# A hybrid decoder step on one core: another order of work in the first stage

## The chip, the core and the metric

The kernel runs on one core of a Trainium2 chip. The core has a tensor engine (PE, with its weight loads shown apart as PEld), a vector engine (DVE), a scalar engine (ACT, also called ScalarE), GpSimd (POOL) and a queue engine (SP), and 16 DMA engines that all queues share. Each engine works through its own list of instructions in order and waits at semaphores for the others. The metric is the device time of one execution in microseconds: 1053.73 us, the median of three runs (1053.68 to 1057.52).

## What is computed

One layer of a decoder, for 512 prompt tokens and 8 x 4 sample tokens; 544 columns in all, and 1024 features.

```python
def trunk_layer(x, c, mixer, lp):
    ada = jnp.einsum('bd,dn->bn', jax.nn.silu(c), lp['w_ada']) + lp['b_ada']
    sh_m, sc_m, gt_m, sh_f, sc_f, gt_f = [a[:, None, :] for a in jnp.split(ada, 6, axis=-1)]
    h = rms_norm(x, g[0]) * (1.0 + sc_m) + sh_m
    y, st = mixer(h)                      # one input projection, then two mixers
    x = x + gt_m * rms_norm(y, g[1])
    h = rms_norm(x, g[2]) * (1.0 + sc_f) + sh_f
    a, b = jnp.split(jnp.einsum('btd,df->btf', h, lp['w_ffn_in']), 2, axis=-1)
    x = x + gt_f * rms_norm(jnp.einsum('btf,fd->btd', jax.nn.silu(a) * b, lp['w_ffn_out']), g[3])
```

The mixer projects h to queries, six kinds of keys and values, gates, the two halves of a gated linear unit (glu) and merge gates. One branch is attention over compressed blocks, selected blocks and a window; for the samples the cached pages come from a pool through a page table. The other is a 31-tap convolution over the glu's output. Compressing means a small network over 32 consecutive key or value rows.

## The kernel before

Data lie transposed: features on the 128 partitions, tokens along the columns, so x is eight blocks of 128 x 544. The columns are two halves of 272 (HT); the last 32 are the samples. Products are made in split form: a value is rounded to a high part (ACT: hi, L168), the rest is the low part (DVE: lo, L171), and high x high, high x low and low x high are summed in PSUM. A weight tile of eight 128 x 128 blocks so takes 24 products per half.

Weights come over SP's queue in the order of one table (RING, made by _plan): 8 conditioning tiles (ada), 3 glu tiles, 8 more ada tiles, and then all others. The first 19 use three buffers wraw and five buffers araw. A load is issued as soon as its buffer is free, strictly in the table's order; after the 19 the two tables w1t of the compressing network follow (load_w1, L440).

The order of instructions has two sources. Later stages are events with due times in microseconds of a plan (ev, spawn, L120 to L143), run in the order of these times. Within that, the building layer places instructions on each engine by its own priorities, and an instruction may be pinned behind another on its engine (tc.issue_after).

The first stage (L470 to L576) goes like this. x is loaded, ACT squares it, DVE sums the squares (acc), PE sums over partitions, and rs, the reciprocal root, is made for all columns (rstd_from, L374). Meanwhile ada tiles arrive. conditioning(h), L511, makes half h of shift and scale, for row blocks 4h to 4h+3: eight tiles of four products with silu(c) into one PSUM tile (ada_product), copied by ACT (adaz, L319), turned by PE (L325), bias added by DVE (adaT, L335), and A0 = (1 + scale) x gain (L527). Dummy products (warm, L491), whose results nothing reads, keep PE busy in the waits. rows(k), L555, makes row block k for each half of the columns: DVE xn = x * A * rs (L405), ACT hh = round(xn + shift) (L407), DVE hl = xn + shift - hh (L408). norm_samples (L410) does the samples of four blocks at once. opened(k), L559, makes the 18 products of block k for the first three glu tiles, whose split weights are w0h and w0l, in six PSUM banks held open over all eight blocks. The loop at L567 runs conditioning(1) between the products of blocks 3 and 4.

Gathers run on POOL: load_pages(bq), L446, issues eight indirect DMAs for page group bq, into the tile X. Group 0 stands behind a tiny copy (pace, L550) that reads ada tile 14, so its gathers wait for that tile; group 1 is called at L575 with no such pin. compress_pages (L454) later multiplies the pages of a group with w1t, 16 products for keys and 16 for values.

After the first stage come the other glu tiles (ztile), key and value tiles (kv_tile), the convolution on DVE (conv, L638), and the samples' queries (q_sample, L840: PE, an ACT copy qz, PE again). compress_prompt, L760, copies the prompt's keys and values with 16 ACT instructions into Xc (L773), ordered so that each of 16 positions l is a contiguous block of 64 columns (four heads x 16 blocks), and multiplies them with w1t, Xc being the operand that PE loads (L778).

## Time and profile before

| | |
|---|---|
| median of three runs | 1053.73 us |
| profiled execution | 1054.71 us, span 1052.9 us |
| PE busy | 1015.9 us (96%) |
| DVE, ACT, POOL busy | 726.8, 529.5, 169.3 us |
| first 50 us: PE, DVE, ACT busy | 44.3, 18.1, 15.9 us |
| first 50 us: DMA share, rate | 0.97, 363 GB/s |
| 50 to 240 us: PE, DVE, ACT busy | 175.9, 138.4, 66.1 us |
| fourth glu tile's first product | 69.35 us |

The profile names an instruction by its line, engine and operation and by its tiles, out<-in. An fp32 product shows as two records. A bracket at the end of a row is the idle time of the engine ahead of the instruction, and what ended it. PE's busy time counts pipelined products and dummies alike, so it doesn't tell how far PE got; the start times of certain products do.

### The profile page before, as it was taken

Reading aid. Unit: us, or ns where it says so; the run is one execution under the profiler, and the core shown is the slowest. Engines: PE = TensorE matmul, PEld = TensorE weight load, DVE = VectorE, ACT = ScalarE, POOL = GpSimd, SP = SyncE. Lnnn points to the kernel's source line nnn. Section 1 sums busy time; section 2 is a strip of 40 time slices with the busy share of each in tenths; the row PEclk is TensorE's granted clock in tenths of the full one; section 3 lists DMA queues with packets and bytes.
Section 4 is the critical chain, followed back from the end, with each engine's and each line's share of the span. In section 5 each row is a group of like instructions: output and inputs, shape, how many; then the busy total and the mean of one; then the engine's idle time right before and its main releaser. Section 6 shows DMA issues by size and latency. Waiting matters only on the chain.

```text
span 1052.9 us, 21049 instructions
## 1 busy us (share of the span) xinstructions
PE 1015.9 (96%) x8454; PEld 918.6 (87%) x8454; DVE 726.8 (69%) x1351; ACT 529.5 (50%) x1169; POOL 169.3 (16%) x175
## 2 busy tenths in 40 slices
PE   8889899899999999999999899999999999999996
PEld 7789788799986787777787499999999999999996
DVE  2469989334386677676765767899888888544644
ACT  3242112646555455654643556765666666544442
POOL 4331530000225243353431000000000000000000
PEclk9999999999999999999999999999999999999998
DMA  9943685433624524424334555655233333555652
GB/s 341 376 151 100 216 263 180 149 115 84 210 62 145 176 99 151 152 99 165 123 120 152 187 184 183 195 190 168 93 101 101 101 101 101 212 181 169 205 178 87
DMA packets 50001, 167.55 MB, mean 159 GB/s; under 512 B 6208, under 2 KB 8400, under 8 KB 49520
## 3 DMA queue, kind: packets, MB, share of 16 engines
q1 hardware_dynamic: 36432, 122.57, 34.8%
q0 software_dynamic: 6272, 22.42, 6.5%
q10 hardware_dynamic: 7200, 21.22, 5.6%
q8 instruction: 66, 1.08, 0.4%
q14 instruction: 31, 0.25, 0.1%
HBM read 149.38 MB, written 16.81 MB: 158 GB/s over the span
## 4 chain that ended last, share of the span: by engine, by line
PE 78%; DVE 10%; DMA 6%; ACT 3%; issue 2%; POOL 1%; SPq 0%; ACTq 0%; DVEq 0%
PE mm L165 48%; PE big L165 10%; PE pv L165 9%; DVE cy L658 6%; PE pt L165 5%; PE big L1083 4%; DMA wraw<-in_wall_dram 3%; DMA araw<-in_wall_dram 1%; DVE wl L171 1%; ACT Xc L773 1%; DMA X<-in_rows_dram,idx 1%; DMA x<-in_xT_dram 1%; ACT PB L1055 1%; POOL X L431 1%; DMA vw<-in_vwin_dram 1%
## 5 line engine op out<-in xcount | busy, mean ns | idle before, releaser
L168 ACT ACTIVATE wh<-wraw 128x1024 fp32r<-128x1024 f32 (+1 forms) x183 | 166.0, 909 | 181.8 <-PE mm L165 100.8
L171 DVE TENSOR_TENSOR wl<-wraw,wh 128x1024 fp32r<-128x1024 f32 (+1 forms) x135 | 156.2, 1158 | 131.8 <-ACT wh L168 115.4
L165 PE MATMUL mm<-hh,wh 128*128 128x272 f32 (+1 forms) x608 | 172.8, 311 | 4.9 <-ACT zt L740 3.5
L165 PE MATMUL mm<-hl,wh 128*128 128x272 f32 (+1 forms) x608 | 168.3, 304 | 0.0
L165 PEld LDWEIGHTS mm<-hh,wh 128*128 128x128 f32 x608 | 116.7, 192 | 16.5 <-issue 6.4
L165 PEld LDWEIGHTS mm<-hl,wh 128*128 128x128 f32 x608 | 116.2, 191 | 5.6 <-issue 2.6
L165 PE MATMUL mm<-hh,wl 128*128 128x272 f32 (+1 forms) x608 | 100.5, 303 | 0.0
L165 PEld LDWEIGHTS mm<-hh,wl 128*128 128x128 f32 x608 | 85.8, 190 | 5.8 <-issue 2.8
L1055 ACT ACTIVATE PB<-big,mx 128x128 f32<-128x128 f32 (+3 forms) x128 | 66.0, 526 | 48.6 <-DVE mx L1052 42.7
L165 PE MATMUL mm<-uh,wh 128*128 128x272 f32 x352 | 90.2, 288 | 0.0
L165 PE MATMUL mm<-ul,wh 128*128 128x272 f32 x352 | 90.1, 288 | 0.0
L658 DVE SCALAR_TENSOR_TENSOR cy<-hist,vc,cy 128x512 f32<-128x512 f32 x120 | 88.0, 789 | 0.4
L165 PE MATMUL mm<-h2h,wh 128*128 128x272 f32 x328 | 77.4, 288 | 0.0
L1063 POOL TENSOR_SCALAR PB<-PB,mx 128x128 f32<-128x128 f32 (+3 forms) x56 | 59.6, 1078 | 84.8 <-DVE mx L1060 50.8
L165 PE MATMUL mm<-h2l,wh 128*128 128x272 f32 x260 | 66.5, 287 | 0.0
L165 PEld LDWEIGHTS mm<-uh,wh 128*128 128x128 f32 x352 | 66.4, 189 | 0.0
L165 PEld LDWEIGHTS mm<-ul,wh 128*128 128x128 f32 x352 | 66.2, 188 | 0.0
L165 PEld LDWEIGHTS mm<-h2h,wh 128*128 128x128 f32 x328 | 58.5, 188 | 0.0
L165 PE MATMUL mm<-h2h,wl 128*128 128x272 f32 x312 | 53.3, 288 | 0.5 <-ACT pv L1550 0.5
L165 PE MATMUL mm<-uh,wl 128*128 128x272 f32 x352 | 52.2, 288 | 0.0
L1052 DVE TENSOR_REDUCE mx<-big 128x2 f32<-128x256 f32 (+3 forms) x64 | 50.6, 815 | 0.4
L165 PEld LDWEIGHTS mm<-h2l,wh 128*128 128x128 f32 x260 | 48.9, 188 | 0.0
(481 smaller groups left out, 2273.0 us busy)
## 6 DMA issues: line engine op xcount, KB each, us to landing
wraw<-in_wall_dram SPq DMA_DIRECT2D x174, 512.0 KB, 4.2
araw<-in_wall_dram SPq DMA_DIRECT2D x12, 512.0 KB, 10.3
wraw<-in_wall_dram SPq DMA_DIRECT2D x16, 384.0 KB, 3.6
xraw<-in_wall_dram SPq DMA_DIRECT2D x8, 512.0 KB, 6.3
kw<-in_kwin_dram ACTq DMA_DIRECT2D x8, 512.0 KB, 3.6
out_wk_dram<-kw ACTq DMA_DIRECT2D x8, 512.0 KB, 4.6
vw<-in_vwin_dram ACTq DMA_DIRECT2D x8, 512.0 KB, 3.5
out_wv_dram<-vw ACTq DMA_DIRECT2D x8, 512.0 KB, 2.6
```

Source lines behind the costliest of these rows:

```text
L165: pe.matmul(out, lhsT, rhs, start=start, stop=stop, **more)
L168: act.activation(dst, src, AF.Copy, scale=scale)
L171: (eng or dve).tensor_sub(dst, src, h.bitcast(F32))
L431: pool.indirect_dma_start(out=X[:, pg], out_offset=None, in_=rows2, in_offset=bass.IndirectOffsetOnAxis(ap=idx[:, 0, col:col + 1], axis=0))
L658: dve.scalar_tensor_tensor(y, hist[:, ct, k:k + TP], w, y, op0=OP.mult, op1=OP.add)
L773: act.activation(o, src[:, r], AF.Copy)
L1052: dve.tensor_reduce(mx[:, 0, r, 2 * jj:2 * jj + 2], sc[:, :, :w], axis=AX.X, op=OP.max, negate=True)
L1055: act.activation(P[r][:, :, j * 128:j * 128 + 128], sc[:, jp, :w].rearrange("p (k n) -> p k n", n=128), AF.Exp, bias=mx[:, 0, r, j:j + 1], ...
L1063: (dve if r or g == 3 and i > 1 else pool).tensor_scalar(v, v, m[:, j:j + 1], None, op0=OP.mult)
L1083: pe.transpose(p[:, x, j * 128:j * 128 + 128], P[r][:, kt, j * 128:j * 128 + 128], ident)
```

## The change

In the first stage:

- x is multiplied by the root in place, once, before any block of rows (eight DVE products of 544 columns).
- ACT then makes hh straight from x, as round(A * x + shift), and DVE makes the same value unrounded (xt) for the low part. The samples' block drops its product with the root.
- conditioning(h) is cut into cond_tile(h, k) and cond_end(h). The tiles of the second half are called behind the blocks' products: two behind block 0, three behind block 1, two behind block 2, one behind the rows of block 3, whose products are pinned behind the second half's turning on PE (issue_after). Then blocks 4 to 7 follow.
- Dummy products go: nine ahead of the first half, three each behind its tiles 1 to 3, and all ten of the second half.
- load_pages(1) stands behind the last gather of load_pages(0), so also behind the pace copy.

Xc is laid out by head and token, so ACT writes 256 contiguous columns per copy, and PE's operand for position l takes every 16th column. Some due times of the plan move, by up to 6 us of the plan; the convolution's taps are spaced 0.966 instead of 1.196.

```diff
-        def conditioning(h):
-            p = P_pt()
-            for k in range(8):
-                raw, tag = take("ada", 8 * h + k)
-                ada_product(p, k, raw)
-                if h and k == 6:
-                    paced(0, raw[:, 0:1])
-                if h == 0 and 0 < k < 7:
-                    warm(3, raw[:, 0:128])
-                raw_done(tag)
-            z = ada_quarters(p)
-            wb = pw if h == 0 else P_pv()
-            warm(3, raw[:, 0:128], wb[:, 0:128])
-            ada_first(h, z)
-            warm(7, z[:, 0:128], wb[:, 0:128])
+        def cond_tile(h, k):
+            if k == 0:
+                cond[h] = P_pt()
+            raw, tag = take("ada", 8 * h + k)
+            ada_product(cond[h], k, raw)
+            if h == 0 and 3 < k < 7:
+                warm(3, raw[:, 0:128])
+            if h and k == 6:
+                paced(0, raw[:, 0:1])
+            if h == 0 and k == 7:
+                warm(3, raw[:, 0:128])
+            raw_done(tag)
+
+        def cond_end(h):
+            z = ada_quarters(cond[h])
+            turned = ada_first(h, z)
+            if h == 0:
+                warm(7, z[:, 0:128])
...
-        warm(9, wt)
-        conditioning(0)
+        for k in range(8):
+            dve.tensor_mul(x0[:, k], x0[:, k], rs)
+        for k in range(8):
+            cond_tile(0, k)
+        cond_end(0)
...
             with tc.issue_after(pool.tensor_copy(pace[:, bq:bq + 1], seen).ins):
-                load_pages(bq)
+                last = load_pages(bq)
+            with tc.issue_after(last):
+                load_pages(bq + 1)
...
-            for hf in range(2):
-                norm_rows(p0, k, hf, x0[:, k], rs, A0, adaT[:, 0], hh, hl, hS)
+            a, sh = A0[:, k, 0:1], adaT[:, 0, k, 0:1]
+            xt = p0.tile([128, TP], F32, name="xt", tag="xt", bufs=2)
+            dve.tensor_scalar(xt, x0[:, k, 0:TP], a, sh, op0=OP.mult, op1=OP.add)
+            for sl in (slice(0, HT), slice(HT, TP)):
+                act.activation(hh[:, k, sl], x0[:, k, sl], AF.Identity, bias=sh, scale=a)
+                dve.tensor_sub(hl[:, k, sl], xt[:, sl], hh[:, k, sl].bitcast(F32))
...
-        for h in range(2):
-            if h:
-                conditioning(1)
-            for k in range(4 * h, 4 * h + 4):
-                rows(k)
-                if k == 4 * h:
-                    norm_samples(p0, k, x0, rs[:, T - NS:], A0, adaT[:, 0], hh, hl, hS[:, k:k + 4])
+        for k, (a, b) in enumerate(((0, 2), (2, 5), (5, 7), (7, 8))):
+            block(k)
+            if k < 3:
                 opened(k)
-        load_pages(1)
+            for j in range(a, b):
+                cond_tile(1, j)
+        with tc.issue_after(cond_end(1)):
+            opened(3)
+        for k in range(4, 8):
+            block(k)
+            opened(k)
...
-        spawn(t, conv(ct, max(t, 40.379 + 29.131 * ct), 1.196))
+        spawn(t, conv(ct, max(t, 40.379 + 29.131 * ct), 0.966))
...
-        Xc = xp.tile([128, 2, 16, 64], F32, name="Xc", tag="X1")
+        Xc = xp.tile([128, 2, 4, 256], F32, name="Xc", tag="X1")
...
-                    src = zts[kd, pr][64 * h2:64 * h2 + 64, 0:TP].rearrange("p (b l r) -> p r b l", b=16, r=2)
+                    src = zts[kd, pr][64 * h2:64 * h2 + 64, 0:TP].rearrange("p (t r) -> p r t", r=2)
                     for r in range(2):
-                        o = Xc[64 * r:64 * r + 64, kd, :, g * 16:g * 16 + 16].rearrange("p l b -> p b l")
+                        o = Xc[64 * r:64 * r + 64, kd, g]
                         act.activation(o, src[:, r], AF.Copy)
         yield t + 26.409
         p = P_pt()
+        Xl = Xc.rearrange("p k g (b l) -> p k l (g b)", l=16)
         for l in range(16):
             for kd in range(2):
-                mm(p[64 * kd:64 * kd + 64, 0:128], Xc[:, kd, l], w1t[kd][:, l], l == 0, False)
+                mm(p[64 * kd:64 * kd + 64, 0:128], Xl[:, kd, l], w1t[kd][:, l], l == 0, False)
```

What this does to the engines' lists shows at three places. The first is POOL at the gathers (X) of the first stage; before:

```order
L484 MEMSET h1v 128x1024
L580 MEMSET QB 128x512
L431 DMA X<-in_rows_dram,idx 128x512 x8
L550 COPY pace<-araw 128x1
L431 DMA X<-in_rows_dram,idx 128x512 x8
```

With the change, at the same place of POOL's list:

```order
L484 MEMSET h1v 128x1024
L612 MEMSET QB 128x512
L559 COPY pace<-araw 128x1
L430 DMA X<-in_rows_dram,idx 128x512 x16
L622 MEMSET Vn 128x512
```

The eight gathers that stood ahead of the pace copy now stand behind the eight others.

The second place is PE at the second half's conditioning. There pt<-araw,cs and pt<-wraw,cs are ada products, mm and big the open glu banks, pt<-c,adaz is the turning, and pv<-wraw,hl and pv<-adaz,hl are dummies. Before, from the end of block 3 to the first products of block 4:

```order
L165 MATMUL big<-hl,w0h 128x272 x4
L165 MATMUL pt<-wraw,cs 32x256 x3
L165 MATMUL pt<-araw,cs 32x256 x8
L165 MATMUL pt<-wraw,cs 32x256 x4
L165 MATMUL pt<-araw,cs 32x256 x8
L165 MATMUL pt<-wraw,cs 32x256 x4
L165 MATMUL pv<-wraw,hl 128x128 x3
L325 MATMUL pt<-c,adaz 128x128 x2
L165 MATMUL pv<-adaz,hl 128x128 x7
L165 MATMUL mm<-hh,w0h 128x272
L165 MATMUL big<-hh,w0h 128x272 x2
```

With the change, from within block 2 to the first products of block 3:

```order
L165 MATMUL mm<-hh,w0l 128x272
L165 MATMUL pt<-wraw,cs 32x256 x4
L165 MATMUL mm<-hh,w0l 128x272
L165 MATMUL big<-hh,w0l 128x272 x4
L165 MATMUL mm<-hl,w0h 128x272 x2
L165 MATMUL big<-hl,w0h 128x272 x4
L165 MATMUL pt<-araw,cs 32x256 x8
L165 MATMUL pt<-wraw,cs 32x256 x4
L325 MATMUL pt<-c,adaz 128x128 x2
L165 MATMUL mm<-hh,w0h 128x272 x2
L165 MATMUL big<-hh,w0h 128x272 x4
```

The ada products of the second half stand between the blocks, the dummies are gone, and a whole block of products follows the turning.

The third place is PE where the first page products (pv<-X,w1t) stand. Before, that was within block 4:

```order
L165 MATMUL mm<-hh,w0h 128x272
L165 MATMUL mm<-hh,w0l 128x272
L165 MATMUL pv<-X,w1t 128x128
L165 MATMUL mm<-hh,w0h 128x272
L165 MATMUL big<-hh,w0h 128x272 x2
```

With the change it is behind block 7, ahead of the fourth glu tile (mm<-hh,wh):

```order
L165 MATMUL mm<-hl,w0h 128x272 x2
L165 MATMUL big<-hl,w0h 128x272 x4
L165 MATMUL pv<-X,w1t 128x128 x3
L165 MATMUL mm<-hh,wh 128x272
L165 MATMUL mm<-hl,wh 128x272
```

PE now meets the wait for the pages after the eight blocks instead of within the fifth.

More of the change, by code (lines that the diff above doesn't have):

```diff
@@ L83, in _plan @@
     p += [(2.345 + 0.1 * n, "ada", n) for n in range(8, 16)]
-    p += [(43.845 + 6.5 * (n - NG), "glu", n) for n in range(NG, 8)]
-    p += [(76.23 + 10.0 * n, "kv", n) for n in range(12)]
+    p += [(45.319 + 6.5 * (n - NG), "glu", n) for n in range(NG, 8)]
+    p += [(76.23 + 9.965 * n, "kv", n) for n in range(12)]
     p += [(60.955 + 4.999 * n, "ada", 16 + n) for n in range(16)]
-    p += [(at(3, 1.759 + 0.428 * n), "ada", 32 + n) for n in range(16)]
+    p += [(at(3, 1.759 + 0.403 * n), "ada", 32 + n) for n in range(16)]
     p += [(164, "g", 0)]
     p += [(205.225 + 3.412 * n, "pw2", n) for n in range(8)]
-    p += [(114.6 + 9.999 * n, "qs", n) for n in range(8)]
+    p += [(114.6 + 9.994 * n, "qs", n) for n in range(8)]
     p += [(TA + 6.539 * n, "q", n) for n in range(2)]
@@ L337, in ada_first @@
                            ada_bias(part)[:, :, 2 * h:2 * h + 2, None].to_broadcast([128, 2, 2, 9]))
+        return ins
     def ada_part(part, bank):
@@ L352, in turn @@
         def turn(z):
-            dve.tensor_add(adaT[:, part].rearrange("p (q a) b -> p a q b", a=2), ada_turned(z),
+            dve.tensor_add(adaT[:, part].rearrange("p (q a) b -> p a q b", a=2), ada_turned(z)[1],
                            ada_bias(part)[:, :, :, None].to_broadcast([128, 2, 4, 9]))
@@ L394, in rstd_from @@
             act.activation(d, p[:, :HT], AF.Copy) if h == 0 else dve.tensor_copy(d, p[:, :HT])
-    first = []
     def norm_rows(pl, k, hf, x, rs, A, S, dst_h, dst_l, keep=None):
@@ L430, in gather @@
             col = bq * 8 + pg
-            pool.indirect_dma_start(out=X[:, pg], out_offset=None, in_=rows2,
+            ins = pool.indirect_dma_start(out=X[:, pg], out_offset=None, in_=rows2,
                                     in_offset=bass.IndirectOffsetOnAxis(ap=idx[:, 0, col:col + 1], axis=0))
+        return ins.ins
     cx = ExitStack()
@@ L448, in load_pages @@
             Xs.append((m2p, xp)[bq % 2].tile([128, 8, 512], F32, name="X", tag=("m2", "X1")[bq % 2]))
-        gather(Xs[bq], bq, pages)
+        return gather(Xs[bq], bq, pages)
     h1k = xp.tile([128, 4, 8, 16], F32, name="h1k")
@@ L509, in body @@
             dve.tensor_add(selq, selq, ident[:, q:q + 32])
-        def conditioning(h):
-            p = P_pt()
-            for k in range(8):
-                raw, tag = take("ada", 8 * h + k)
-                ada_product(p, k, raw)
-                if h and k == 6:
-                    paced(0, raw[:, 0:1])
-                if h == 0 and 0 < k < 7:
-                    warm(3, raw[:, 0:128])
-                raw_done(tag)
-            z = ada_quarters(p)
-            wb = pw if h == 0 else P_pv()
-            warm(3, raw[:, 0:128], wb[:, 0:128])
-            ada_first(h, z)
-            warm(7, z[:, 0:128], wb[:, 0:128])
+        cond = {}
+        def cond_tile(h, k):
[15 more added lines that the diff above has]
+                warm(7, z[:, 0:128])
             r = slice(4 * h, 4 * h + 4)
-            first.append(dve.scalar_tensor_tensor(A0[:, r], adaT[:, 1, r], 1.0, gains[:, 0, r, None].to_broadcast([128, 4, 9]),
-                                     op0=OP.add, op1=OP.mult))
+            dve.scalar_tensor_tensor(A0[:, r], adaT[:, 1, r], 1.0, gains[:, 0, r, None].to_broadcast([128, 4, 9]),
+                                     op0=OP.add, op1=OP.mult)
+            return turned
         last = sq
@@ L565, in opened, with block @@
                         mm(gl[f][hf][:, :HT], w[:, k], r[:, k, sl], k == 0 and part == 0, k == 7 and part == 2)
[L567 to L575 removed]
+        def block(k):
+            rows(k)
+            if k % 4 == 0:
+                samples(k)
+        for k, (a, b) in enumerate(((0, 2), (2, 5), (5, 7), (7, 8))):
+            block(k)
+            if k < 3:
+                opened(k)
+            for j in range(a, b):
[5 more added lines that the diff above has]
+            opened(k)
         split_upto(rst["use"])
@@ L910, in body @@
         ada_part(part, half_big)
-    spawn(150, gate_tile())
+    spawn(151.16, gate_tile())
     cyhl = []
-    spawn(100, layer_norm(LN))
+    spawn(100.001, layer_norm(LN))
     m2h = []
@@ L1401, in body @@
     for n, ft in enumerate(KEPT + (0, 1, 2, 3, 4)):
-        ev(TO + 26.151 + 2.961 * n if n < 3 else when("out1", ft), out_tile, 1, ft, n == 0, n == 7)
+        ev(TO + 25.84 + 2.961 * n if n < 3 else when("out1", ft), out_tile, 1, ft, n == 0, n == 7)
     spawn(TO + 24.407, second_norm(0, TO + 24.715, 0.806))
-    spawn(TO + 47.393, second_norm(1, TO + 49.67, 1.875))
+    spawn(TO + 47.163, second_norm(1, TO + 49.886, 1.875))
     run_until(TO + 48.1)
```

57 lines of the change are left out of this document (33 added, 24 removed).

## Prediction

> **What bounds the kernel now.** I read the busy time by stretch first, then the chain of waits over the first 80 us, then the queues that feed it. By stretch (start:end, length, busy time of PE, weight loads, DVE, ACT and POOL with counts, granted clock, DMA share, GB/s):
>
> ```profile
> 20.00:30.00 10.00, 8.43 (x85) 5.08 (x83) 0.00 (x0) 0.00 (x0) 0.00 (x0) 1.00 1.03 406
> 30.00:40.00 10.00, 7.25 (x49) 5.63 (x46) 8.67 (x20) 5.65 (x10) 0.00 (x0) 0.91 1.02 402
> 50.00:240.00 190.00, 175.93 (x1561) 163.50 (x1554) 138.37 (x217) 66.11 (x137) 39.86 (x33) 0.97 0.51 168
> 240.00:390.00 150.00, 147.77 (x1270) 123.64 (x1270) 91.45 (x211) 82.60 (x216) 41.29 (x46) 1.00 0.39 127
> ```
>
> After 240 us PE is busy 98.5% of the time: nothing is to be had there but work. The first 40 us are another kernel: the DMA engines are full (share 1.0, 400 GB/s) while DVE and ACT do nothing at all from 20 to 30. The chain of waits (start, length, what) says on what:
>
> ```profile
> 9.74 15.32 DMA araw<-in_wall_dram
> ...
> 29.49 0.57 PE pt L165 x8
> ...
> 51.24 7.34 DMA X<-in_rows_dram,idx
> ...
> 58.67 0.77 PE pv L165 x2
> ...
> 68.90 0.69 ACT at L615 x2
> ```
>
> PE waits for the fifth conditioning tile (issued 9.74, landed 25.06), later for a gathered page (landed 58.58). POOL, which issues the gathers, tells which gather was where (start, length, instruction; in brackets the idle time before it):
>
> ```profile
> 7.66 1.04 POOL L431 DMA_INDIRECT X<-in_rows_dram,idx  x1 [4.24 <-DVE selq L507]
> ...
> 17.22 0.95 POOL L431 DMA_INDIRECT X<-in_rows_dram,idx  x1 [0.30 <-issue]
> 41.89 0.41 POOL L550 COPY pace<-araw 128x1 f32<-128x1 f32 x1 [23.72 <-DMA araw<-in_wall_dram]
> 42.46 0.97 POOL L431 DMA_INDIRECT X<-in_rows_dram,idx  x1 [0.16 <-DVE hl L408]
> ...
> 51.24 0.95 POOL L431 DMA_INDIRECT X<-in_rows_dram,idx  x1 [0.30 <-issue]
> ```
>
> Eight gathers run at 7.66 to 18.2, eight more behind the pace copy. Only the load behind the copy is page group 0; so the early eight are group 1, which nothing needs before group 0. They land among the conditioning weights that PE waits for.
>
> **Term 1, the second gather later: 5.0 us.** Moved by the weight queue (q1) and the gather queue (q0), as packets, MB and share; the first row is 0 to 12 us, the other two 0 to 24 us:
>
> ```profile
> q1 hardware_dynamic: 1402, 2.69, 63.5%
> ...
> q1 hardware_dynamic: 2139, 5.37, 60.1%
> q0 software_dynamic: 668, 2.10, 26.6%
> ```
>
> From 12 to 24 us the weights got 2.68 MB and the gather nearly all of its 2.1: 0.397 MB/us together. Without the gather the fifth tile is there 2.08 / 0.397 = 5.2 us sooner, at 19.8. From below the gain is zero, if tiles were held up by their eight buffers and not by bandwidth; but the DMA share of 1.0 excludes idle queues. PE's sums for the root now stand behind the first product of tile 0; that tile is the queue's bytes up to 2.8 MB, and 2.69 had gone by 12 us, so I allow 0 to 1 us, most of it beside the wait for the fifth tile. I take 5.0: the first half's last product ends at 25.1 instead of 30.06 (29.49 + 0.57 in the chain). Multiplying x by the root ahead costs DVE 8 x 0.725 us (the 128x544 add, below) = 5.8 us, from 18.5 to 24.3, in the stretch where DVE is empty; without that cover it is 5.8 us on the path.
>
> ```profile
> L503 DVE TENSOR_TENSOR acc<-acc,sq 128x544 f32<-128x544 f32 x6 | 4.3, 725 | 0.7 <-ACT sq L499 0.2
> L656 DVE TENSOR_SCALAR cy<-hist,vc 128x512 f32<-128x512 f32 x4 | 2.2, 540 | 0.0
> L678 DVE TENSOR_TENSOR cy<-cy,lrs 128x272 f32<-128x272 f32 x8 | 3.0, 436 | 0.1
> ```
>
> **Term 2, from that product to the fourth glu tile: 39.3 us before, 31 after.** The points on the way (start, length, engine, line):
>
> ```profile
> 30.13 0.38 ACT L319 ACTIVATE adaz<-pt 128x256 f32<-128x256 f32 x1 [12.78 <-PE pt L165]
> 31.51 0.20 DVE L527 SCALAR_TENSOR_TENSOR A<-adaT,vc 128x36 f32<-128x36 f32 x1
> 35.68 1.21 DVE L171 TENSOR_TENSOR w0l<-araw,w0h 128x1024 fp32r<-128x1024 f32 x1
> 38.12 0.57 PE L165 MATMUL mm<-hh,w0h 128*128 128x272 f32 x1 [1.53 <-ACT hh L407]
> 39.62 1.11 PE L165 MATMUL big<-hh,w0l 128*128 128x272 f32 x4
> 40.75 1.04 PE L165 MATMUL big<-hl,w0h 128*128 128x272 f32 x4
> 42.89 0.41 PE L165 MATMUL mm<-hl,w0h 128*128 128x272 f32 x2
> 43.64 0.41 PE L165 MATMUL mm<-hh,w0h 128*128 128x272 f32 x2
> 51.49 0.38 ACT L319 ACTIVATE adaz<-pt 128x256 f32<-128x256 f32 x1 [9.85 <-PE pt L165]
> 54.23 0.39 PE L165 MATMUL mm<-hh,w0h 128*128 128x272 f32 x1
> 69.35 0.39 PE L165 MATMUL mm<-hh,wh 128*128 128x272 f32 x1
> ```
>
> Before, PE ran the first half's rows, then the second half's conditioning alone, then stood or ran dummies from 51.4 to 54.2, waited 2.9 us for X, and ran the rest. After, by DVE's order: A 1.65 us behind the last product (31.71 - 30.06), then xt 0.54, one sample product 0.28, w0l 1.21, two differences 0.84, a sample sum 0.28, w0l 1.21, xt 0.54, w0l 1.21: 7.8, call it 7.9 us to the third w0l, at 33.0. Before it was 6.8, but the rows behind it kept PE to 38.12, 8.06 us after. From there PE has 132 glu products at 0.125 us (six in 0.75 us from 42.89), 16.5; 29 conditioning products at 0.14 (four, recorded as x8, in the 0.57 us of the chain), 4.1; one wait for adaz, about 1.1; three page products, 0.4. Nothing else: the second chain of adaT, A and first rows (51.49 to 54.23, 2.7 us) lies beside row block 3, 18 products or 2.25 us, and ScalarE makes that block's rows straight from x and A. Sum 30.0 us. If PE runs cold once, as it did from 38.12 (five products from 39.62 to 40.75, 0.226 us each, for 3.3 us), 1.7 more. I take 31.0, for the stretch to 33.0 is as full of waits as before: the fourth glu tile at 56.1. DVE keeps up: a row block costs 0.54 + 0.84 = 1.4 us there, PE 2.25.
>
> The page wait is now at the end of the opening, and has its own clock. Conditioning tile 14 can be issued only when the third w0l frees its buffer, at 33.0; landing takes 4.2 us (the median of the page's DMA issues) to 6.7 (the least in the full stretch), so 37.2 to 39.7;
>
> ```profile
> wraw<-in_wall_dram SPq DMA_DIRECT2D x174, 512.0 KB, 4.2
> ...
> DMA to landing us min/median/max: 6.7/10.3/17.1
> ```
>
> From that landing to the last page of group 0 it was 58.58 - 41.89 = 16.7 us: 53.9 to 56.4, and 0.4 us of products. Both clocks end within a microsecond. I take **56.3, that is 13.0 us earlier** than 69.35.
>
> [...]
>
> **Term 3, what the 16 gathers in one row hold up: nothing.** POOL now issues from 38 + 0.6 for 16 x 1.26 us, to 58.8. Behind stand Vn's memset, four convolution loads and the first tap product:
>
> ```profile
> 69.42 3.73 POOL L605 DMA_DIRECT2D hst<-in_conv_dram  x4
> 73.76 2.73 POOL L646 TENSOR_TENSOR cpr<-hst,vc 128x992 f32<-128x992 f32 x1 [0.60 <-DMA hst<-in_conv_dram]
> 82.48 1.09 DVE cy L650
> ```
>
> Loads at 59.3, tap product 63.6 to 66.4; DVE's sum (last row, from the chain) came 13.1 us after the fourth glu tile, so it will ask at 69.4. 3 us to spare; a POOL that is later than that delays DVE's taps one for one. Group 1 lands near 66; its first product comes some 25 us of PE work after the fourth glu tile. Weights that follow share 0.51 of the DMA engines.
>
> **Term 4, Xc in whole rows: 1.9 us.**
>
> ```profile
> L773 ACT ACTIVATE Xc<-zt 64x256 f32<-64x256 f32 x16 | 10.3, 644 | 0.2
> L319 ACT ACTIVATE adaz<-pt 128x256 f32<-128x256 f32 x2 | 0.8, 384 | 22.6 <-PE pt L165 22.6
> ...
> 201.75 0.42 PE L165 MATMUL pt<-selq,qz 128*128 128x32 f32 x2 [4.66 <-ACT qz L853]
> L165 PEld LDWEIGHTS pt<-w1t,Xc x64: 133/137/137, 225.1 to 228.4; 128*64 128x64 f32 x64
> ```
>
> ScalarE takes 644 ns for 256 columns written 256 bytes apart, where 256 contiguous ones take 384. The copies still read every other element, so each costs between 384 and 644: 0 to 4.2 us. They stand ahead of qz, for which PE idles 4.66 us, so what is saved is PE's. I take 3.4 (half of the stride stays cheap). In return PE loads Xc's columns 64 bytes apart: 64 loads at a pitch of 3.3 / 64 = 0.05 us, no change or twice as long (ScalarE's own ratio is 1.7), 0 to 3.5 us; I take 1.5.
>
> [...] No row here shows a strided load.
>
> The other numbers of the plan move single instructions by one or two places; where PE is 98.5% busy they are worth 0, with 3 us to either side.
>
> **Sum.** The profiled execution took 1054.71 us (span 1052.9), 1.0 above the median. 1054.7 - 13.0 - 1.9 = 1039.8; I predict **1039.5** for the median, 14 us less than 1053.7. Everything behind the opening has nearly the same order, is bound by PE and DVE at once and starts as a whole when the opening ends, so I carry the 13 us in full.
>
> **Rivals.**
> A. The early gather cost nothing: the tiles were held back by their eight buffers. Then term 1 falls to about 0 and the rest stays: 1045. Against it: the full DMA share. Chance 0.12.
> B. Pages are the new bound. Gather 0 now shares with w1t and three weight tiles; if PE's wait at the end of the opening is 5 to 6 us, the gain ends at 8: 1046. For it: the two clocks meet already. Chance 0.13.
> C. Swallowed behind the opening. DVE, busy 138 of the 190 us up to 240, has the convolution's taps now spaced at 0.966 instead of 1.196, so weight splits stand behind more taps and PE waits for them; the order puts the fourth split 2 us of DVE work later. Four such waits take 10 us: 1050. Chance 0.10.
> [...] Chance 0.05.
>
> My forecast keeps 0.60. A change of 0.5%, 5 us, is about what a measurement of this kernel can tell from none, so below 1048.5 is faster: 0.60 + 0.12 + 0.13 and a little of C, 0.87; same 0.08; slower 0.05. Range 1031 to 1049: downward both opening bounds (2 us), Xc in full (2) and the plan's 3; upward A, B and half of C.
>
> **What would show it.** The fifth tile's product near 20 us and the first half's end near 25; POOL with no gather before 37; no dummy stretch between conditioning and block 4; the fourth glu tile at 55 to 57.5; a PE wait for X below 2 us; Xc copies near 0.43 us and PE's wait for qz near 1. I am wrong if the fourth glu tile starts after 61, or if it starts at 56 and attention (before: first at 240) has not moved by as much.

## The result, and the profile after

The changed kernel takes 1041.11 us (median of four runs, 1040.92 to 1042.87) where the kernel before took 1054.76 (four runs): a ratio of 0.987, 95% interval 0.9847 to 0.9894. Forecast were 1039.5 and 1031 to 1049. The profiled execution took 1041.11 us with a span of 1039.3, 13.6 less than the 1052.9 before. A later chip gave 1042.46, and one gave 1056.28, no better than the kernel before there; the experiments come to that.

The sum was nearly right, and its terms were not. First the busy time by stretch of the kernel after (columns as in the prediction):

```profile
20.00:30.00 10.00, 10.00 (x93) 6.30 (x85) 6.29 (x13) 1.68 (x3) 0.00 (x0) 0.80 0.90 329
30.00:40.00 10.00, 8.73 (x54) 6.13 (x53) 8.26 (x18) 5.78 (x11) 0.00 (x0) 0.83 0.91 308
50.00:240.00 190.00, 184.27 (x1659) 173.47 (x1659) 142.85 (x220) 73.56 (x162) 49.34 (x40) 0.99 0.54 182
```

DVE now works from 20 to 30 us, and PE never waits there, but the granted clock is 0.80. Also, PE is busy 184.3 of the 190 us up to 240, for 175.9 before: a gain that the forecast had small (the page wait of 2.92 us, which is gone, is part of it). The chain of waits (start, length, what) has lost the landing of the fifth conditioning tile; what stands in its place is PE itself:

```profile
6.15 7.41 DMA wraw<-in_wall_dram
13.70 0.59 PE pt L165 x2
14.29 2.13 PE mm L165 x24
16.42 0.56 PE pt L165 x6
17.00 2.79 PE mm L165 x12
19.79 3.57 PE pt L165 x32
...
27.39 0.57 PE pt L165 x8
```

The fifth tile does come early. By the row of its transfer (durations in ns; issued at 10.17), it lands at 10.17 + 9.8 = 20.0, for 25.06 before:

```profile
L236 SPq DMA_DIRECT2D araw<-in_wall_dram x1: 328/328/328, 10.2 to 10.2; - x1
DMA to landing us min/median/max: 9.8/9.8/9.8
```

The products of tile 0 stand around the root's sums and wait for that tile until 13.6; the root's own products take 2.79 us, for 1.54 before; four conditioning tiles take 3.57, that is 0.22 us a product for the 0.14 I had counted. The last product of the first half ends at 27.39 + 0.57 = 27.96.

The points on the way, by the timeline (start, length, engine, line):

```profile
22.28 1.08 PE L165 MATMUL pt<-araw,cs 128*32 128x256 f32 x8
...
33.91 1.22 DVE L171 TENSOR_TENSOR w0l<-araw,w0h 128x1024 fp32r<-128x1024 f32 x1
40.37 0.19 POOL L559 COPY pace<-araw 128x1 f32<-128x1 f32 x1 [36.95 <-DMA araw<-in_wall_dram]
58.47 0.83 PE L165 MATMUL pv<-X,w1t 128*128 128x128 f32 x6
59.17 0.39 PE L165 MATMUL mm<-hh,wh 128*128 128x272 f32 x1
61.77 0.97 POOL L430 DMA_INDIRECT X<-in_rows_dram,idx  x1 [0.30 <-issue]
68.67 2.37 POOL L678 TENSOR_TENSOR cpr<-hst,vc 128x992 f32<-128x992 f32 x1 [1.62 <-DVE cy L690]
72.84 1.18 DVE L682 TENSOR_REDUCE cy<-cpr 128x32 f32<-128x992 f32 x1
...
235.59 0.29 PE L165 MATMUL mm<-cyl,wh 128*128 128x272 f32 x1
```

The first row is the fifth conditioning tile. The third w0l ends at 35.1, the fourth glu tile starts at 59.17, with no wait for the pages ahead of it. The last row is the first product with the low part of the convolution's result, a point that every version passes; before, it came at

```profile
252.72 0.29 PE L165 MATMUL mm<-cyl,wh 128*128 128x272 f32 x1
```

These two points cut the kernel into three stretches, which are measured the same way in every trace below: to the fourth glu tile 69.35 before and 59.17 after (-10.2); from there to the low part's product 252.72 - 69.35 = 183.4 and 235.59 - 59.17 = 176.4 (-7.0); from there to the end of the span 1052.9 - 252.72 = 800.2 and 1039.3 - 235.59 = 803.7 (+3.5). The forecast had -13.0, -1.9 and 0.

The instructions around Xc (median of the three durations in ns, first and last start):

```profile
L165 PEld LDWEIGHTS pt<-w1t,Xc x64: 195/210/226, 210.8 to 214.5; 128*64 128x64 f32 x64
L805 ACT ACTIVATE Xc<-zt x16: 426/432/451, 177.7 to 184.6; 64x256 f32<-64x256 f32 x16
```

The median copy went from 638 to 432 ns (the mean from 644 to 433). A strided weight load takes 210 ns where one of whole rows took 137, but the 64 loads follow each other over 3.7 us where they did over 3.3: the loads, 64 x 0.210 = 13.4 us in all, overlap each other and the products (210.8 to 214.6, by the same view), so their price is 0.4 us together.

### The profile page after: what moved, and what is told of

The parts are those of the page before. It is cut to its first block, busy times and chain, and to the rows that moved or that the text cites. A ratio compares the mean times of both kernels' runs of the same rounds, so it can differ in the third digit from the quotient of the medians.

```text
span 1039.3 us, 20942 instructions
## 1 busy us (share of the span) xinstructions
PE 1011.1 (97%) x8398; PEld 910.9 (88%) x8398; DVE 730.6 (70%) x1349; ACT 528.4 (51%) x1169; POOL 171.4 (16%) x175
## 4 chain that ended last, share of the span: by engine, by line
PE 85%; DVE 7%; DMA 5%; ACT 2%; issue 1%; SPq 0%; ACTq 0%; DVEq 0%
PE mm L165 51%; PE big L165 12%; PE pv L165 11%; PE pt L165 6%; DVE cy L690 4%; DMA wraw<-in_wall_dram 4%; PE big L1116 4%; DVE wl L171 1%; DMA xraw<-in_wall_dram 1%; DMA vw<-in_vwin_dram 0%; PE big L1244 0%; DVE cy L682 0%; ACT wh L168 0%; DMA c<-in_cst_dram 0%; ACT PB L1088 0%
```

## The experiments

Twelve runs followed on four chips, each beside the kernel before on its own chip; after2 and after3 are the changed kernel itself. Single executions of one kernel spread by 2 to 13 us, by chip, so medians tell a few us at best; the profiles tell more. Where a stretch is named, it is one of the three above, read from one execution of each kernel.

| kernel | to glu tile 4 | to low part | to the end | span of the profile | ratio to before, 95% |
|---|---|---|---|---|---|
| before | 69.35 | 183.4 | 800.2 | 1052.9 | |
| b_gather | 71.09 | 180.9 | 800.2 | 1052.2 | 1.0022 (1.0002 to 1.0042) |
| b_xc | 69.15 | 176.7 | 799.9 | 1045.8 | 0.997 (0.9954 to 0.9986) |
| after | 59.17 | 176.4 | 803.7 | 1039.3 | 0.987 (0.9847 to 0.9894) |
| a_early | 61.56 | 177.1 | 805.4 | 1044.0 | 0.9889 (0.9854 to 0.9924) |
| a_warm9 | 58.55 | 175.7 | 804.1 | 1038.3 | 0.9896 (0.9868 to 0.9924) |
| after2 | 73.78 | 175.5 | 805.6 | 1054.8 | 1.0002 (0.9972 to 1.0032) |
| a_fill | 70.49 | 176.7 | 803.8 | 1050.9 | 0.9981 (0.9961 to 1.0001) |
| a_oldxc | 68.42 | 180.6 | 806.5 | 1055.5 | 1.0028 (1.0005 to 1.0052) |
| a_oldlate | 77.02 | 178.0 | 800.5 | 1055.5 | 0.9957 (0.9941 to 0.9973) |
| after3 | 59.19 | 177.1 | 804.4 | 1040.7 | 0.9902 (0.987 to 0.9934) |
| a_best | 59.54 | 180.7 | 802.8 | 1043.0 | 0.9878 (0.9844 to 0.9911) |
| a_oldplan | 59.78 | 176.1 | 800.1 | 1035.9 | 0.9835 (0.9812 to 0.9857) |
| a_oldplan_early | 61.38 | 177.1 | 799.9 | 1038.3 | 0.987 (0.9844 to 0.9895) |

Of the twelve, b_gather, b_xc, a_early and a_warm9 ran on one chip; after2, a_fill, a_oldxc and a_oldlate on a second; after3 and a_best on a third; the last two on a fourth.

### The gather's move, alone and undone

The kernel before with this one edit:

```diff
             with tc.issue_after(pool.tensor_copy(pace[:, bq:bq + 1], seen).ins):
-                load_pages(bq)
+                last = load_pages(bq)
+            with tc.issue_after(last):
+                load_pages(bq + 1)
...
-        load_pages(1)
```

> The kernel before with one edit: the second page group's eight gathers are issued behind the first group's eight, none at 7.66 us. Theory of the prediction (bytes set the first stage): the fifth conditioning tile lands 5.2 us sooner and all that follows moves with it, 1049.5. Theory from the trace after (PE sets it): six tiles with three dummy products each take 1.43 us apiece, so with both tile waits gone (0.61 + 0.96 us) the first half still ends at 28.4 instead of 30.06; the pages' own clock hangs on the third w0l and moves by the same 1.7; 1053.0, between 1051.5 and 1053.7. Rival A of the prediction (the early gather cost nothing): 1054.7, the first half's last product still near 30.

And the kernel after with the edit taken back:

```diff
-            with tc.issue_after(last):
-                load_pages(bq + 1)
...
             opened(k)
+        load_pages(1)
```

> The kernel after with the early gather back (the second page group at 7.66 us, nothing else moved). If the weights that it displaces are what PE waits for: the fifth tile lands at 25 again instead of being ready at 22.3, the first half ends 2.5 to 2.8 us later, 1043.7. If the page clock is worth something too (eight gathers less behind the pace copy, group 0 alone with the weights), less than that: 1042 to 1043. If the prediction's 5.0 us are right: 1046. If the early gather cost nothing: 1041.1.

Alone, the move won nothing: 1057.01 us (ten runs) beside 1053.38 (nineteen), above all three times of the expectation. The timeline of b_gather has the first half's last product at

```profile
29.57 0.64 PE L165 MATMUL pt<-araw,cs 128*32 128x256 f32 x8
```

And PE's waits in its opening (us in total, times, longest):

```profile
PE pv L165 <- DMA X<-in_rows_dram,idx: 5.2, 1, 5.2
PE mm L165 <- ACT hh L407: 1.8, 2, 1.5
```

The first half ends at 30.2, as it did before (30.06). The fifth tile landed at 9.98 + 10.0 = 20.0, as in the kernel after, and the waits for tiles are gone; but PE needs the time for dummies and, for 3.4 us (below), at half clock. Without that loss of 1.7 us the half would have ended at 28.5, an estimate, near the 28.4 of the expectation. Further on, the wait for X is 5.2 us, where it was 2.9. So the weights did land sooner, and nothing in the old order used it. Why the median is even above the kernel before is not shown: the profiled execution took 1053.98 us at a mean clock of 0.990, and those above 1056 us had 0.981 to 0.987. In the new order the move is worth something: with it undone the first half waits for its fifth tile again, and the opening ends 2.4 us later than at 59.17. From the timeline of a_early:

```profile
24.97 1.08 PE L165 MATMUL pt<-araw,cs 128*32 128x256 f32 x8 [0.30 <-DMA araw<-in_wall_dram]
...
61.56 0.39 PE L165 MATMUL mm<-hh,wh 128*128 128x272 f32 x1
```

The last pair of kernels repeats this on another chip: 61.38 against 59.78, 1.6 us (3.7 by the medians of the whole kernel). Part of it is the clock: at the first half's end that pair is 0.8 us apart (30.10 and 29.28), and from 34 to 44 us the granted clock was 0.83 with the early gather and 1.00 without it. In place of 5.0 the move is worth 1.6 to 2.4 us in the opening, and nothing by itself; the other 8 us come from the rest of the first stage's edit (above all, it seems, the second half of the conditioning inside the first half's products), whose parts were not run one by one.

### The half clock in the first stage

The kernel after with the dummies around the root again:

```diff
-        rstd_from([acc, last], (rs[:, :HT], rs[:, HT:]), 1024, (P_mm, P_mm))
+        rstd_from([acc, last], (rs[:, :HT], rs[:, HT:]), 1024, (P_mm, P_mm)); warm(9, wt)
```

> The kernel after with nine dummy products added behind the root (they stand ahead of the root's sums, between these and the root's products, and behind them), and with that tile 0's product behind the root again; the nine dummies behind tiles 1 to 3 stay away. If a cold clock and tile 0 ahead of the root hold the first half to 27.96: the clock stays at 1.00 from 14 to 24 us, the root's products take 1.54 us instead of 2.79, the fifth tile's product starts at 20.9 and the first half ends at 25.8; 2.1 us less, 1039.0. If the dummies cost as much as they save, or if the pages land no sooner and PE then waits for X: 1041. If the prediction's own 25.1 comes: 1038.3.

And with three dummies ahead of each of the two sets of sums as well:

```diff
         for m, a in enumerate(accs):
+            if mid: mid()
...
-rstd_from([acc, last], (rs[:, :HT], rs[:, HT:]), 1024, (P_mm, P_mm))
+rstd_from([acc, last], (rs[:, :HT], rs[:, HT:]), 1024, (P_mm, P_mm), lambda: warm(3, wt)); warm(9, wt)
```

> The kernel after with dummy products throughout the root: two or three ahead of its sums, three between its sums, three behind them and six behind its products. With nine dummies fewer ahead and between, the clock had still fallen to half at 16.7 us, 3.4 us after the stretch of one-column sums began at 13.3. If that thin stretch is what lowers the clock: 1.00 from 14 to 24 us, the root's products in 1.5 us, the first half's end at 26.0 to 26.5 for 27.96 (0.8 us of it paid for the dummies between the sums) and the fourth glu tile at 57.5; 1.5 to 2 us less than the kernel after. If the pages hold the opening's end instead, PE waits for X by as much and nothing is won. If it is something other than PE's own load: the clock falls at the same place.

The busy time of the stretch from 14 to 24 us tells; the granted clock is the third number from the end. The kernel after:

```profile
14.00:24.00 10.00, 9.99 (x79) 6.92 (x78) 4.27 (x8) 0.66 (x2) 0.00 (x0) 0.66 0.92 348
```

The same program in another execution, after3:

```profile
14.00:24.00 10.00, 10.00 (x75) 7.22 (x74) 3.05 (x6) 0.66 (x2) 0.00 (x0) 0.56 0.81 316
24.00:34.00 10.00, 9.15 (x78) 6.54 (x70) 6.26 (x15) 4.35 (x7) 0.00 (x0) 0.93 0.90 332
```

b_gather, with the old dummies:

```profile
14.00:24.00 10.00, 10.00 (x88) 8.61 (x91) 1.12 (x4) 0.66 (x2) 0.00 (x0) 0.83 0.78 307
```

a_warm9, with nine dummies:

```profile
14.00:24.00 10.00, 10.00 (x86) 8.15 (x85) 5.36 (x10) 0.66 (x2) 0.00 (x0) 0.66 0.76 298
```

a_oldxc (below), whose first stage is that of the kernel after:

```profile
14.00:24.00 10.00, 9.99 (x94) 6.97 (x93) 4.62 (x9) 0.66 (x2) 0.00 (x0) 0.83 0.98 370
```

a_fill, with six more:

```profile
14.00:24.00 10.00, 10.00 (x113) 8.25 (x113) 5.51 (x10) 0.66 (x2) 0.00 (x0) 1.00 0.92 347
```

And a_best (below), with the same dummies as a_fill:

```profile
14.00:24.00 10.00, 10.00 (x76) 9.16 (x79) 3.97 (x8) 0.66 (x2) 0.00 (x0) 0.66 0.75 296
```

Taken by half microseconds, the clock of the kernel after is 1.00 up to 17.0 us, 0.61 in the next half, 0.50 in each one from 17.5 to 23.5, 0.56 in one more and then 1.00. At 0.50 for t us, a mean over 10 us is 1 - 0.05 t. So the array ran at half rate for 3.4 us in b_gather and a_oldxc (0.83), 6.8 in after, a_warm9 and a_best (0.66), and 8.8 + 1.4 = 10.2 in after3 (0.56 and 0.93): one, two and three times 3.4. The same first stage had one, two and three of them in different executions, and the same dummies gave none in a_fill and two in a_best.

What such a stretch costs shows in that first stage. The last product of the first half, in a_oldxc, the kernel after and after3:

```profile
25.78 0.64 PE L165 MATMUL pt<-araw,cs 128*32 128x256 f32 x8
```

```profile
27.32 0.64 PE L165 MATMUL pt<-araw,cs 128*32 128x256 f32 x8
```

```profile
28.66 0.64 PE L165 MATMUL pt<-araw,cs 128*32 128x256 f32 x8
```

The half ends at 26.4, 27.96 and 29.3 with one, two and three; on a_oldxc's own chip, after2 and a_oldlate ended it at 27.4 and 27.6 with two. So each costs 1.0 to 1.5 us, and with none the end would be near 25, an estimate, which is the 25.1 of the forecast. In a_fill, with none and fifteen dummies more, the root's products took 1.54 us and the half ended at 26.5, as expected.

The nine dummies of a_warm9 missed: clock 0.66 again, an opening 0.6 us shorter for the 2.1 expected, and a median of 1043.11 us. With a_fill's, the expectation on the clock came in, and then not on the next chip. So the fall lasted 3.4, 6.8 or 10.2 us where it came, its start differs from one execution to the next (17.1 us in the kernel after, 16.2 in after2 and 15.2 in after3, the same program), and dummies around the root don't prevent it reliably: none in a_fill, 6.8 us in a_best. What starts it, and what sets the three lengths, is not shown.

### Xc alone, and undone

The kernel before with the new layout, and the kernel after with the old one; the first:

```diff
-        Xc = xp.tile([128, 2, 16, 64], F32, name="Xc", tag="X1")
+        Xc = xp.tile([128, 2, 4, 256], F32, name="Xc", tag="X1")
...
-                        o = Xc[64 * r:64 * r + 64, kd, :, g * 16:g * 16 + 16].rearrange("p l b -> p b l")
+                        o = Xc[64 * r:64 * r + 64, kd, g]
...
-                mm(p[64 * kd:64 * kd + 64, 0:128], Xc[:, kd, l], w1t[kd][:, l], l == 0, False)
+                mm(p[64 * kd:64 * kd + 64, 0:128], Xl[:, kd, l], w1t[kd][:, l], l == 0, False)
```

> The kernel before with the one edit that Xc is copied in whole rows and read with a stride. By the prediction 3.4 of the copies' time is saved and 1.5 lost in the loads: 1.9 less, 1052.8. By the trace after, where the strided loads cost 0.15 to 0.3 us together and PE no longer waits for qz at all: 3.4 to 4.7 less, 1050 to 1051.3. If other work takes the place of that wait (the convolution's taps, weight splits on DVE): 1054.7.

> The kernel after with Xc laid out as before (copies that write 256 bytes apart, loads that read whole rows). By the prediction 1.9 us more. By the traces, which put 3.4 us of copies, and a half-rate stretch of 3.7 us behind the 4.66 us wait for qz, on it: 4.5 to 6.5 more, with the wait for qz back and a granted clock under 0.8 behind it. If the other numbers around that stage do the work: 0 to 1 more.

The medians: b_xc 1050.64 beside 1053.38; a_oldxc 1060.85 beside after2's 1056.28 on the same chip, 4.6 more. Both differ from the forecast's 1.9, but not beyond the noise: the interval of b_xc's gain is 1.5 to 4.8 us, and single executions on a_oldxc's chip spread by 11 to 13. In the second stretch of the profiles: 183.4 and 180.9 with the old layout in the old kernel, 176.7 with the new; 180.6 with the old in the new kernel, where nine others have 175.5 to 178.0 and a_best (below) 180.7. That makes 2.6 to 6.6 us. Some 1.7 of the 6.6 are not Xc's: the profiled kernel before also ran at half rate for 3.4 us behind an earlier wait (granted clock 0.57 from 130 to 134 us, 1.00 in b_xc). So 2.6 to 5 us are left, more than 1.9 in every pair of profiles. The waits and the clock say why. In a_oldxc the timeline shows

```profile
198.23 0.41 PE L165 MATMUL pt<-selq,qz 128*128 128x32 f32 x2 [2.77 <-ACT qz L885]
```

and the busy time by stretch

```profile
195.00:200.00 5.00, 2.23 (x13) 2.01 (x12) 0.71 (x1) 4.82 (x10) 0.00 (x0) 0.86 0.22 82
200.00:205.00 5.00, 5.00 (x45) 4.65 (x44) 1.74 (x2) 1.73 (x3) 0.00 (x0) 0.80 0.36 130
```

PE waits 2.8 us for qz, behind the copies, and then runs at half rate for a while: (0.14 + 0.20) x 5 / 0.5 = 3.4 us of it, 1.7 lost. In the kernel before the wait was 4.66, and behind it, by the same view,

```profile
200.00:205.00 5.00, 3.25 (x15) 3.25 (x16) 1.22 (x1) 3.38 (x8) 0.00 (x0) 0.70 0.00 0
```

the clock was 0.70 as well, 3.0 us at half rate. In b_xc, by the tile's instructions,

```profile
L165 PEld LDWEIGHTS pt<-w1t,Xc x64: 186/206/230, 217.9 to 221.6; 128*64 128x64 f32 x64
L773 ACT ACTIVATE Xc<-zt x16: 426/432/445, 187.7 to 194.6; 64x256 f32<-64x256 f32 x16
```

and there is no wait for qz at all. The copies' 3.4 us cover the whole wait of a_oldxc, and with it goes the half clock that followed; where the other 1.3 us of the 4.66 went is not shown. So the copies gained (638 to 432 ns) and the loads paid (137 to 206 here), as the prediction took it. But a copy did not come down to the 384 ns that 256 contiguous columns took. The price on the loads shows in the single load (210 for 137 ns) and hardly in their row (3.7 for 3.3 us).

### The end of attention

In the third stretch every kernel with the new numbers of the plan has 803.7 to 806.5 us, for about 800 with the old ones (a_best, with old ones, has 802.8, and 2.8 us of the waits for weights shown below). The kernel after with the old numbers from there on:

```diff
-    p += [(at(3, 1.759 + 0.403 * n), "ada", 32 + n) for n in range(16)]
+    p += [(at(3, 1.759 + 0.428 * n), "ada", 32 + n) for n in range(16)]
...
-    p += [(TO + 31.9 + 2.718 * n, "out1", n) for n in range(5)]
+    p += [(TO + 31.9 + 3 * n, "out1", n) for n in range(5)]
```

(and thirteen more of that kind, all behind it.)

> The kernel after with the numbers of the plan from the end of attention on (conditioning tiles 32 to 47, output projection, second norm, feed-forward) as before. If they gave back what the opening had won (17.0 us ahead at the last group of attention, 13.6 at its end): three waits for conditioning weights of 3.3 us fall to about 1.2 at the same place, the clock stays at 1.00 there, and the kernel ends 2.5 to 3.4 us sooner than the kernel after. If the waits come from earlier transfers whatever the numbers: no change. If the new numbers are worth what they were set for later on: slower by up to 2.

Third stretch 800.5, for 805.6 in after2 beside it: 5.1 us; median 1053.22 beside 1056.28, although its opening was the longer one in the profile. PE's waits for weights from 540 to 615 us, in the kernel after:

```profile
PE mm L165 <- DMA wraw<-in_wall_dram: 4.4, 4, 1.6
```

and in a_oldlate:

```profile
PE mm L165 <- DMA wraw<-in_wall_dram: 1.0, 2, 0.7
```

In the kernel after three of the four waits for conditioning weights fall within 5 us, and the clock goes, by the busy time of stretches of 2 us:

```profile
572.00:574.00 2.00, 0.81 (x12) 0.33 (x16) 2.00 (x3) 2.00 (x7) 0.00 (x0) 0.87 0.74 244
574.00:576.00 2.00, 2.00 (x14) 1.19 (x11) 1.09 (x4) 0.71 (x3) 0.00 (x0) 0.50 0.73 215
576.00:578.00 2.00, 2.00 (x12) 1.25 (x11) 0.52 (x1) 0.60 (x1) 0.00 (x0) 0.78 0.84 274
```

Conditioning tiles set closer (0.403 for 0.428), so that PE asks for weights sooner than they land, would fit. The waits for weights differ by 3.4 us, but with the old numbers PE waits for ACT in the same place: over the whole third stretch all rows of PE's waits add up to 9.8 us in the kernel after and 8.8 in a_oldlate. That leaves 1.0 us of waits. Half rate for 2 x (0.13 + 0.50 + 0.22) / 0.5 = 3.4 us costs 1.7 more; together 2.7 of the 3.2 us between these two third stretches. In after2 a second such half-rate stretch follows (granted clock 0.57 from 637 to 641 us). So more of the loss is clock than waiting. Which of the fifteen changed lines does it was not tried.

### The same program on another chip

> The changed kernel itself, beside the three edits of it that follow, on their chip. 13 to 14 us below the kernel before if what was measured first holds; its profile is a second look at the same program: the half-rate stretch at 17 to 24 us and the three waits for conditioning weights at 568 to 574 us should be there again if they belong to the program and not to one execution.

The kernel after took 1056.28 us there (ten runs), as much as the kernel before (1057.05, twenty-six runs). All four kernels profiled on that chip have the long opening, 68 to 77 us. The timeline of after2:

```profile
45.16 0.61 PE L165 MATMUL pt<-wraw,cs 128*32 128x256 f32 x8
58.91 0.95 POOL L430 DMA_INDIRECT X<-in_rows_dram,idx  x1 [0.30 <-issue]
59.12 0.38 ACT L319 ACTIVATE adaz<-pt 128x256 f32<-128x256 f32 x1 [23.93 <-remote]
59.56 0.69 PE L325 MATMUL pt<-c,adaz 128*128 128x128 f32 x2 [13.78 <-issue]
```

The last conditioning product is over at 45.77 by its record. ACT's copy, which waits for it and nothing else that the profile shows, starts at 59.12, and PE's turning behind it at 59.56: 13.8 us of nothing, which is nearly all of the 14.6 that this opening is longer than 59.17. SP's next weight load, which waits for the same product to free its buffer, resumes at 59.11. This stand of PE ends as the row of sixteen gathers ends (59.86), which here go out without a pause, every 1.26 us. In a_oldlate the stand was 16.4 us, and it ended at 62.3, 3.2 us after that kernel's row (58.12 + 0.94 = 59.06):

```profile
62.30 0.69 PE L325 MATMUL pt<-c,adaz 128*128 128x128 f32 x2 [16.36 <-ACT adaz L319]
```

In a_fill it was 3.2 us at that place and 8.4 in pieces behind it, in a_oldxc 3.2 and 3.6 in pieces; in both, PE was back before 46.8, in the middle of the row. So the two ends fall together in one kernel of four.

To see whether the long row is the cause, the next kernel has it broken in two, along with the dummies of a_fill and the old late numbers:

```diff
                 last = load_pages(bq)
-            with tc.issue_after(last):
-                load_pages(bq + 1)
...
             act.activation(at_[:, hf * HT:hf * HT + HT], p, AF.Copy, scale=0.5)
+            if ct == 0 and hf == 0:
+                with tc.issue_after(pool.tensor_copy(pace1, at_[:, 0:1]).ins):
+                    load_pages(1)
```

> The changed kernel once more, as a base for the next one on the same chip. Two chips so far: on one its opening ended at 59.2 us (first product of the fourth glu tile) and the kernel took 1041, on another PE stood 13.8 us behind the last conditioning product while the sixteen gathers ran, the fourth glu tile came at 73.8 and the kernel took 1056. Either may come: 1041 with no such stand, or 1053 to 1056 with one that ends as the row of gathers ends.

> The kernel after with three edits: the dummies around the root that kept the clock at 1.00; the plan's numbers from the end of attention on as before; and the second group's eight gathers taken out of the row of sixteen, issued behind the first glu evacuation near 59 us. Sum from the traces so far: opening 57.5 to 58.5, 176.5 from the fourth glu tile to the first product of the convolution's second part, 800.2 from there to the end, span 1034 to 1036, 1036 to 1038 in all. If the row of sixteen is what made PE stand on the slow chip: no stand behind 52 us here even where the kernel after has one, and 15 to 20 less than it there. If the first eight gathers are enough for it, or if that chip holds up any dense opening: PE stands here too, the fourth glu tile comes past 65, and 1044 to 1050. The dummies or the old numbers alone did not remove it: it was there with either.

The third chip had no such stand: after3 took 1042.46 us with its opening at 59.19, the first case of its expectation. So a_best tells nothing on the cause, and whether a broken row would help stays open. For itself it missed: 1041.25 us, not 1036 to 1038. The profiled execution is its slowest (1044.73). What that one lost shows in the timeline, on POOL and DVE:

```profile
75.14 2.15 POOL L682 TENSOR_TENSOR cpr<-hst,vc 128x992 f32<-128x992 f32 x1
79.56 1.17 DVE L686 TENSOR_REDUCE cy<-cpr 128x32 f32<-128x992 f32 x1
```

The eight late gathers stand ahead of the convolution's first tap product, which starts at 75.1 for 68.7, and DVE's sum comes at 79.6 for 72.8. PE also waits 3.6 us for a weight tile (xraw) where it waited 0.6 to 0.8, and then runs at half rate (granted clock 0.51 from 137 to 143 us). The second stretch is 180.7, about 4 us longer.

### The first stage and Xc without the other numbers

Every other number of the plan as before, and the same with the early gather:

```diff
-    p += [(45.319 + 6.5 * (n - NG), "glu", n) for n in range(NG, 8)]
-    p += [(76.23 + 9.965 * n, "kv", n) for n in range(12)]
+    p += [(43.845 + 6.5 * (n - NG), "glu", n) for n in range(NG, 8)]
+    p += [(76.23 + 10.0 * n, "kv", n) for n in range(12)]
...
-        spawn(t, conv(ct, max(t, 40.379 + 29.131 * ct), 0.966))
+        spawn(t, conv(ct, max(t, 40.379 + 29.131 * ct), 1.196))
```

(and all others of the change's kind.)

> Only the first stage and Xc are changed; every other number of the plan is as before. From the traces so far, in three stretches: opening to the fourth glu tile's first product 59.2, or 68 to 77 on a chip where PE stands behind the conditioning; from there to the first product of the convolution's second part 176.5 if the first stage and Xc do it all, 178 to 180 if the plan's numbers there are worth something; from there to the end 799.9 to 800.5 as in every kernel with the old late numbers but one, where the new ones gave 803.7 to 806.5. Where PE doesn't stand: span 1036, 1037.7 in all, 3 to 4 below the change itself; if the new numbers are worth what the prediction allowed either way: 1041 or more.

> The same with the second page group back at 7.66 us, so eight gathers behind the pace copy and no row of sixteen; nothing else moves. Where PE doesn't stand with the row of sixteen: the opening ends 2.4 us later, as it did with the early gather in the kernel after (61.6 for 59.2), and so does the kernel: 1040. On a chip where it stands: if the row of sixteen is the cause, the opening ends at 62 here for 68 to 77 beside it, and this kernel is 6 to 15 faster than its neighbour; if eight are enough or the chip holds up any dense opening, no better than its neighbour.

Both came near the first case, on a chip without the stand: a_oldplan 1037.28 us (1036.54 to 1038.44, for 1037.7), ratio 0.9835, below the change itself (0.987, the intervals overlap a little, and the two never ran on one chip); a_oldplan_early 1041.0 (for 1040). The three stretches of a_oldplan are 59.78, 176.1 and 800.1. So all of the moved numbers together won nothing in the middle and lost at the end of attention, where a_oldplan's waits for weights are again

```profile
PE mm L165 <- DMA wraw<-in_wall_dram: 1.0, 2, 0.6
```

It is the fastest version tried. It keeps the row of sixteen gathers, and was not run on the chip where PE stood.

## Why the prediction was right, and where it wasn't

The time was within 1.6 us by luck: an opening that won less, a middle that won more and an end that lost balanced out, -10.2 - 7.0 + 3.5 for -13.0 - 1.9 + 0. Of the signs that were named, three missed: the fifth tile's product (22.28, not near 20), the first half's end (27.96, not near 25) and the fourth glu tile (59.17, not 55 to 57.5).

**Term 1 failed.** The step was "the fifth tile is there 5.2 us sooner, at 19.8 ... the first half's last product ends at 25.1". The tile did come, at 20.0. But I let PE follow at once. PE got to the fifth tile only at 22.28 (root's products 2.79 us for 1.54, four tiles in 3.57 us at half rate), and the end came at 27.96: 2.1 us, not 5.0. The allowance for tile 0 ahead of the sums (0 to 1 us) was right: they start at 14.22 for 13.30. What I had left out was the clock in this place; I had priced one cold stretch (1.7 us) and put it behind the third w0l, where one came too (0.83 from 30 to 40 us). That the clock is what failed shows in the same first stage with one, two and three half-rate stretches: 26.4, 27.96 and 29.3. The bytes gave 1.6 to 2.4 us when the edit was undone, and none when done alone.

**Term 2 held.** From the first half's end to the fourth glu tile I had 31.0; it was 59.17 - 27.96 = 31.2. The third w0l came 7.2 us behind the product (7.9), and the page wait did not show, where the two clocks were said to end within 1 us of each other. DVE's root product lies hidden from 20.4 to 25.5, as term 1 had said (18.5 to 24.3).

**Term 3 held** on the kernel after: DVE's first sum of the taps came 13.7 us behind the fourth glu tile (I had 13.1), so POOL's row of sixteen cost nothing there. Its condition, that a later POOL delays the taps one for one, is what a_best ran into. But the term asked only what the row holds up behind it on POOL; on one chip PE stood while the row was issued, and nothing in the profile of before pointed to that.

**Term 4 was mis-sized.** No run shows the ground that I gave for 3.4, that half of the stride stays cheap; what the runs showed is the copy itself, 644 ns before and 433 after (mean), and 16 x 0.211 = 3.4 us saved. Loads: 0.4 us, not 1.5. And the wait for qz that went took a half-rate stretch along, which I hadn't priced though its rows stood in the trace. 2.6 to 5 us in all.

**The plan's numbers** I had at 0, with 3 to either side. They are 0 in the middle and cost 3.5 to 6.5 us at the end of attention, which is beyond the bound. "Carry the 13 us in full" failed there, not behind the opening: a_oldplan carries all it wins to the end.

**Rivals.** A's cause (tiles held back by their buffers) didn't occur: with the gather moved the fifth tile lands 5.1 us sooner in either order. Its price came all the same in the old order, which used none of it, and a third to a half of it in the new one. B didn't occur: no wait for X. C didn't occur, the taps at 0.966 changed nothing that can be seen. A slower kernel (chance 0.05) didn't occur: PE ran at half rate for 6.8 us from 14 to 24 us and 3.4 from 30 to 40, 10.2 of the opening's 59.17. None of them foresaw the chip on which the gain was gone.

## What to carry to other kernels

Taking a transfer out of the way is worth only what the engine behind it can use (here the tile came 5.1 us sooner, and the opening won nothing in the old order and 1.6 to 2.4 us in the new): read when that engine would get there at the clock that it will have, not when the bytes land. In the kernel before, three waits of PE, of 2.9 (X), 2.9 (ACT zt, ending at 129.4) and 4.7 us (qz), each had 3.4 us at half rate behind them (granted clock 0.50 from 59 to 62 us, 0.57 from 130 to 134 and 0.57 from 202 to 206), 1.7 us lost; in b_gather a wait of 2.9 us for zt, ending at 130.9, had none (clock 1.00 from 129 to 135 us). So removing such a wait can pay more than its length (the wait for qz in a_oldxc, 2.8 us and 1.7 more behind it), and three short ones in a row can cost more than their sum (1.6, 1.0 and 0.7 us in the kernel after, the last ending at 573.8, and 1.7 lost at half rate behind them). When a change moves an order and a table of numbers at once, try the old numbers with the new order: here that was the fastest kernel.

## What the runs showed that was not expected

- The half-rate stretches of the first stage last 3.4, 6.8 or 10.2 us, and the same program has different ones in different executions (0.66 against 0.56 in the stretch from 14 to 24 us), which moves the end of the first half by 1.0 to 1.5 us for each 3.4.
- A chip on which the kernel before took 1057.05 us, 2 to 4 above the others, and the kernel after gained nothing: PE, ACT and SP stood 13.8 us behind one product that was over by its record. In that kernel the stand and a row of sixteen gathers end within 1 us of each other; in a_oldlate PE went on 3.2 us after the row, in a_fill and a_oldxc in the middle of it. What makes it is not shown, and no kernel without the row was run on that chip.
- A weight load that reads every 16th column takes 210 ns for 137, and costs 0.4 us in a row of 64; a ScalarE copy of 64 x 256 that writes with a stride of 256 bytes takes 638 ns for 432.
